# Layer 1's MoE: the four experts of a block side by side instead of two and two

## The chip, the core and the metric

The kernel runs on one core of one Trainium2 chip. The metric is the device time of one execution, in microseconds (us). Engines by their names in the profile: TensorE (PE; its weight loads are PEld), VectorE (DVE), ScalarE (ACT), GpSimd (POOL), SyncE (SP, whose queue issues nearly all loads).

## The reference, cut to what matters

Two layers run over 256 context and 256 latent tokens of width 1024. Each has a mixer (attention and a state-space scan) and then a mixture of experts: a router takes the best of 4 groups and the best 2 of its 8 experts. Only the latent tokens pass through layer 1's MoE, since they alone are the output.

```python
def hier_moe(h, rw1, rb1, rw2, rb2, w_gate, w_up, w_down):
    ...
    y = jnp.zeros_like(h)
    for e in range(N_EXPERTS):                       # 32 experts, EXPERT_FF = 256
        y = y + gate[:, e:e + 1] * ((jax.nn.silu(h @ w_gate[e]) * (h @ w_up[e])) @ w_down[e])
    return y
```

After layer 1 a final RMSNorm follows. All is in f32. An expert has 3 MB of weights, so a layer's MoE reads 96 MB.

## The kernel before, in words

The MoE runs over blocks of experts that together fill 128 slots: 2 experts of 64 slots in layer 0 (16 blocks), 4 experts of 32 slots in layer 1 (8 blocks). Function `moe`, from L1390. For each block b:

- `stage_b` (L1567) gathers the tokens of the block by matmuls with a one-hot matrix `PT` and leaves them transposed, in two halves of the width, in `xgT`.
- `stage_c` (L1596, matmuls on L1610) multiplies by gate and up weights. An expert's gate/up weights come in two tiles of 1 MB, one for each half of the width. The slots of an expert are 32 partitions of the PSUM tile, so its matmuls use 32 columns of TensorE's array. In layer 1, part 0 takes both halves of the experts 0 and 1, alternating between the two, and part 1 both halves of the experts 2 and 3.
- `stage_d1` is SiLU times up, `stage_d2` turns the result, `stage_d3` (L1627, matmuls on L1647; the last block L1638) multiplies by the down weights, one tile of 1 MB for each expert, again two experts at a time.
- `stage_y` and `stage_e` (L1656, L1667) scale by the gate, and scatter back to the tokens by matmuls with `P` (L1673, L1674), times the layer's modulation `g2` (L1677), added to the stream `xs` (L1678). `comb[0]` is the running combine of the block before, and `step` takes one of its four parts.
- `slots` (L1520) makes, once in a layer, the slot tables that `P` and the gates are read from. Its one-hot tile `oh` is on the tag `pT`.

The loop of a block is: d1, gather matrices for block b+2, `P`, `stage_b` of block b+1, d2, `stage_c` part 0 of b+1, d3, y, `stage_c` part 1 of b+1, e. The last block is done in `finish` (L1695), with its down weights in half tiles, all first halves ahead of all second halves. At block 5 of layer 1 stands a branch, `fallback` (L1823, the branch on L1828), which is not taken here.

What sets the order: a planner places the instructions on each engine by its own estimate of durations, unless a `manual_schedule` holds an engine to program order. Layer 0's loop holds TensorE so; layer 1's doesn't (`nullcontext`).

Weights: `seq` lists the tiles of a layer in the order of their use (`add_gu`, `add_dn`, L1398 and L1405); a number such as "tile 16" is a place in this list. Tiles 0 to 3 are loaded ahead during the mixer (`XKEY`, `AHEAD`). Six tiles go in quarters of 256 KB into small buffers that other parts of the kernel leave free (`SMALL`: one letter for each quarter's buffer; `QUARTER` and `qload`, L235). All others rotate over 15 buffers of 1 MB (`LOAD_TAGS`: one R, four W, ten B); such a load waits until TensorE has read the tile that was in its buffer before.

Of the kernel before, what the change touches and what calls it, by code (L numbers as in the profile page):

```python
# [13 lines left out]
D = 1024  # L14
# [17 lines left out]
AHEAD = ((1, "B", 1, 0), (3, "B", 0, 1), (3, "B", 1, 1))  # L32
SMALL = ({2: 'ccxx', 3: 'pppq', 4: 'yyqj', 8: 'mmMM'}, {4: 'pppq', 7: 'yyqj', 6: 'ccxx', 10: 'saom', 12: 'MMlh', 16: 'kwtt'})
# [9 lines left out]
LATE = ((15, 16, 17), ())  # L43
# [4 lines left out]
MAN = ((0, 99), (99, 99))  # L48
# [7 lines left out]
EST = ((0, 0, 0), (1, 1, 1))  # L56
# [26 lines left out]
def _tile_kernel(tc, A, out, dbg=None):  # L83
# [151 lines left out]
    def qload(src, tags, after=None):  # L235
        q = []
        for n, a in enumerate(tags):
# [6 lines left out]
            elif a == "l":  # L244
                t = kc[:, KC["le"][0]:KC["le"][0] + 512]
            elif a == "s":
# [748 lines left out]
    def route_out(l, oT):  # L995
# [394 lines left out]
    def moe(l, R):  # L1390
# [125 lines left out]
        for i in LATE[l]:  # L1516
            load(i, gate if gate is not None else idx[:, 0:1])
# [26 lines left out]
        g2 = {}  # L1544
        if l == 0:
            g2t = big("g2")
        for who in ((1, 0) if l == 0 else (0,)):
            if l == 0:
                g2_ = mod_bcast(l, "g2", who, g2t[:, who * 1024:(who + 1) * 1024])
                g2[who] = [g2_[:, 0:512], g2_[:, 512:1024]]  # L1550
            else:
                g2[who] = []
                for h in range(2):
                    g2[who].append(tw("bm", 2, "g2"))
                    a = 64 + 32 * h + who
                    nc.gpsimd.dma_start(g2[who][h], modd[l, 2][a:a + 1, :].to_broadcast([128, 512]))
# [10 lines left out]
        def stage_b(b):  # L1567
            xg = xgs.pop(b)
            h_ = []
            for kk in range(2):  # L1570
# [22 lines left out]
                step(EST[l][0])  # L1593
            xgT[b] = h_

        def stage_c(b, part):  # L1596
# [4 lines left out]
            if per == 2:  # L1601
                todo = [(part, list(range(2)))]
            else:
# [23 lines left out]
        def stage_d3(b):  # L1627
# [13 lines left out]
            for i0 in range(0, per, 2):  # L1641
                w = {i: get("dn", ex[i], 2) for i in (i0, i0 + 1)}
                for h in range(2):
# [132 lines left out]
        for j in range(1, nT):  # L1776
            V.tensor_scalar(tid[:, j, 0:nb], tid[:, 0, 0:nb], -128.0 * j, None, op0=ALU.add)
# [200 lines left out]
```

## Time and profile before

| what | value |
|---|---|
| median of 3 runs | 1104.37 us (1100.53 to 1105.21) |
| the profiled execution | 1102.8 us, of which the span of its records is 1101.0 us |
| TensorE busy | 1009.9 us, 92% of the span, mean granted clock 0.968 |
| VectorE, ScalarE, GpSimd busy | 608.9, 334.8, 355.0 us |
| moved by DMA | 306.21 MB, mean 278 GB/s |
| layer 1's MoE | about 838 to 1101 us of the span |

The median of the runs is 1.6 us above the profiled execution. "Busy" is the share of time in which an engine has at least one instruction in work; matmuls in different column groups of the array overlap, so a mean duration (about 0.6 us for one of these matmuls) is more than the time that each adds. The granted clock is 1.00 for 2.4 GHz and 0.50 for 1.2 GHz. One f32 matmul of the program is two instructions in the trace, and some records are missing.

### The profile page before, as it was taken

The page shows a single profiled execution, that of the slowest core. Times are in us where ns is not written, and L with a number is a line of the kernel's source. Part 1 is how long each engine was busy: PE and PEld are TensorE (multiplying, and loading weights), DVE is VectorE, ACT ScalarE, POOL GpSimd, SP SyncE. Part 2 cuts the span into 40 slices and gives each one's busy share as a digit, 9 for nine tenths or more (in the row PEclk, how much of TensorE's full clock was granted, in tenths as well). Part 3 has the DMA queues.
Part 4 walks back from the last instruction along what each step waited for, and adds up shares of the span by engine and source line. Part 5 has one row for each costly group of instructions (what it writes and reads, how often), then busy time and mean ns, then how long its engine had stood idle before and what let it go on. Part 6 is the DMA issues. An engine that isn't in the chain of part 4 may idle for free. (4 is left out here: it accounts for less than half of the span.)

```text
span 1101.0 us, 14498 instructions
## 1 busy us (share of the span) xinstructions
PE 1009.9 (92%) x5244; PEld 558.0 (51%) x5244; DVE 608.9 (55%) x1351; ACT 334.8 (30%) x688; POOL 355.0 (32%) x366
## 2 busy tenths in 40 slices
PE   5999999999996999999699889999997999899986
PEld 3778554667674344344244357845775344323321
DVE  4596288875785356556445677749864153222222
ACT  4464344544630111111012075434642111101101
POOL 2130134420562467667636431023311011111121
PEclk9999999999986999999899899999997999999998
DMA  9521577787287997999979164475679699898971
GB/s 375 180 77 52 206 261 257 248 335 311 97 295 293 368 367 318 415 418 404 382 283 418 43 235 155 151 288 212 244 269 329 238 388 420 337 372 356 420 265 39
DMA packets 54675, 306.21 MB, mean 278 GB/s; under 512 B 6168, under 2 KB 7064, under 8 KB 22976
## 3 DMA queue, kind: packets, MB, share of 16 engines
q1 hardware_dynamic: 49120, 288.10, 67.0%
q0 software_dynamic: 4224, 15.21, 4.5%
q10 hardware_dynamic: 1248, 1.86, 0.5%
q8 instruction: 44, 0.72, 0.3%
q14 instruction: 39, 0.32, 0.1%
HBM read 300.89 MB, written 4.26 MB: 277 GB/s over the span
## 5 line engine op out<-in xcount | busy, mean ns | idle before, releaser
L1678 POOL TENSOR_TENSOR xs<-xs,tmp 128x512 f32<-128x512 f32 x144 | 180.2, 1281 | 276.4 <-DVE tmp L1677 276.3
L1610 PE MATMUL bk<-we,xgT 128*64 128x512 f32 (+1 forms) x950 | 242.1, 602 | 0.0
L1610 PEld LDWEIGHTS bk<-we,xgT 128*64 128x64 f32 (+1 forms) x950 | 62.7, 125 | 130.4 <-issue 127.9
L1647 PE MATMUL sc<-we,sa 128*64 128x512 f32 (+1 forms) x430 | 106.2, 600 | 0.1
L1663 DVE SCALAR_TENSOR_TENSOR yl<-sc,gs,yh 128x512 fp32r<-128x512 f32 x46 | 34.3, 748 | 113.2 <-ACT yh L1662 112.6
L1662 ACT ACTIVATE yh<-sc,gs 128x512 fp32r<-128x512 f32 x46 | 31.5, 687 | 210.9 <-PE sc L1647 167.7
L1647 PEld LDWEIGHTS sc<-we,sa 128*64 128x64 f32 (+1 forms) x430 | 31.1, 125 | 58.0 <-issue 56.7
L1677 DVE TENSOR_TENSOR tmp<-md,g 128x512 f32<-128x512 f32 x60 | 41.3, 688 | 29.7 <-POOL xs L1678 18.7
L1677 DVE TENSOR_TENSOR tmp<-py,g 128x512 f32<-128x512 f32 x60 | 41.2, 687 | 24.0 <-PE py L1674 13.2
L1616 ACT ACTIVATE sa<-bk 128x256 f32<-128x256 f32 x24 | 9.2, 383 | 136.1 <-PE bk L1610 126.8
L1578 PEld LDWEIGHTS tp<-PT,h 128*128 128x128 f32 x256 | 33.9, 199 | 28.4 <-issue 12.7
L1578 PE MATMUL tp<-PT,h 128*128 128x128 f32 x256 | 41.5, 300 | 5.0 <-DVE PT L1500 1.7
L770 PE MATMUL sc<-kT,qT 128*128 128x512 f32 (+1 forms) x96 | 45.7, 559 | 0.0
L792 PE MATMUL py<-pT,vt 128*64 128x128 f32 x320 | 43.6, 280 | 1.2 <-DVE oT L821 1.2
L1072 DVE TENSOR_TENSOR lo<-wo,hi 128x512 fp32r<-128x512 f32 x44 | 34.4, 785 | 16.2 <-PE sc L1255 8.6
L1584 DVE TENSOR_SCALAR xgT<-tp,a,sh 128x128 f32<-128x128 f32 x32 | 13.0, 409 | 54.1 <-PE tp L1578 47.5
L1582 ACT ACTIVATE xgT<-tp,sh,a 128x128 f32<-128x128 f32 x32 | 14.6, 457 | 91.0 <-PE tp L1578 85.2
L792 PEld LDWEIGHTS py<-pT,vt 128*64 128x64 f32 x320 | 32.5, 136 | 15.4 <-issue 8.2
L401 PE MATMUL bk<-wh,hH 128*128 128x256 f32 (+1 forms) x128 | 39.8, 311 | 0.2
L403 PE MATMUL bk<-wh,hL 128*128 128x256 f32 (+1 forms) x128 | 38.2, 298 | 1.8 <-DVE hL L382 1.7
L774 ACT ACTIVATE p<-sc,mx 128x512 f32<-128x512 f32 (+1 forms) x48 | 29.4, 612 | 33.2 <-DVE mx L772 23.2
L402 PE MATMUL bk<-wl,hH 128*128 128x256 f32 (+1 forms) x128 | 37.8, 295 | 0.0
(421 smaller groups left out, 2146.5 us busy)
## 6 DMA issues: line engine op xcount, KB each, us to landing
we<-wgu SPq DMA_DIRECT2D x111, 1024.0 KB, 11.1
we<-wdn SPq DMA_DIRECT2D x53, 1024.0 KB, 9.8
wl<-wmod SPq DMA_DIRECT2D x22, 1024.0 KB, 4.9
wl<-wm SPq DMA_DIRECT2D x10, 1024.0 KB, 8.2
wo<-wout SPq DMA_DIRECT2D x8, 1024.0 KB, 5.8
we<-wgu SPq DMA_DIRECT2D x31, 256.0 KB, 5.3
ring<-wgu SPq DMA_DIRECT2D x7, 1024.0 KB, 5.8
wm<-wm SPq DMA_DIRECT2D x6, 1024.0 KB, 12.2
```

Source lines behind the costliest of these rows:

```text
L401: T.matmul(o, a[0], b[0], start=start, stop=False)
L402: T.matmul(o, a[0], b[1], start=False, stop=False)
L403: T.matmul(o, a[1], b[0], start=False, stop=stop)
L770: T.matmul(pm[:, 0:nk], qT[:, e, t * 128:(t + 1) * 128], kT[:, e, 0:nk], start=True, stop=True)
L792: T.matmul(py[e * 64:(e + 1) * 64, 0:128], vts[0][:, k, h * 64:(h + 1) * 64], pT[:, k * 128:(k + 1) * 128], start=(k == 0), stop=(k == nk ...
L1072: eng.tensor_tensor(lo, src, hi.bitcast(F32), op=ALU.subtract)
L1578: T.matmul(p_, R["hres"][t][:, c], xg[j], start=(j == 0), stop=(j == nT - 1))
L1610: T.matmul(pg[c], xgT[b][half][:, k, c], w[i][k], start=(half == 0 and k == 0), stop=(half == 1 and k == 3))
L1647: T.matmul(pd[h][c], aT[:, k, c], w[i][2 * k + h], start=(k == 0), stop=(k == 1))
L1663: V.scalar_tensor_tensor(yl, pd[h], gs[:, b:b + 1], yh.bitcast(F32), op0=ALU.mult, op1=ALU.subtract)
L1677: V.tensor_tensor(tmp, pc, g2[1 if t < 2 else 0][h], op=ALU.mult)
L1678: (eng or (V if EADD[l][n] == "V" or alt and n % 2 else G)).tensor_tensor(xs[:, t, hs_], xs[:, t, hs_], tmp, op=ALU.add)
```

## The change

In layer 1, `stage_c` now takes half `part` of all four experts, k by k, so that four matmuls for four column groups follow each other; `stage_d3` does the same with the down weights; `add_gu` lists the tiles in this order. TensorE is held to program order in layer 1's loop too, with layer 0's loop body. In that order `slots` stands after `stage_c(0, 0)` and before `stage_c(0, 1)`. The small buffers are dealt out anew: tile 6 goes to `MMlk`, tile 12 to `ccxx`, and tile 16 to four quarters of `xs`, rows of context tokens that layer 1 no longer needs; these hold tile 0 first, so tile 16 is loaded after `stage_c(0, 0)`. The one-hot tile moves from `pT` to `bm`, the SiLU tile from `pT` to `xp`, the two loads of `g2` go after `slots`, and the combine takes its PSUM banks in threes.

```diff
-AHEAD = ((1, "B", 1, 0), (3, "B", 0, 1), (3, "B", 1, 1))
-SMALL = ({2: 'ccxx', 3: 'pppq', 4: 'yyqj', 8: 'mmMM'}, {4: 'pppq', 7: 'yyqj', 6: 'ccxx', 10: 'saom', 12: 'MMlh', 16: 'kwtt'})
+AHEAD = ((1, "B", 1, 0), (3, "B", 2, 0), (3, "B", 3, 0))
+SMALL = ({2: 'ccxx', 3: 'pppq', 4: 'yyqj', 8: 'mmMM'}, {4: 'pppq', 7: 'yyqj', 6: 'MMlk', 10: 'saom', 12: 'ccxx', 16: 'XYUZ'})
-LATE = ((15, 16, 17), ())
+LATE = ((15, 16, 17), (16,))
...
+            elif a in "XYUZ":
+                t = xs[:, a in "XY", (a in "YZ") * 512:(a in "YZ") * 512 + 512]
...
-                    oht.append(tw("pT", 2, "oh"))
+                    oht.append(tw("bm" if l else "pT", 2, "oh"))
...
         def add_gu(b, part):
             ex = list(range(b * per, (b + 1) * per))
-            if per == 2:
-                seq.extend(("gu", e, part) for e in ex)
-            else:
-                seq.extend(("gu", e, h) for h in range(2) for e in ex[2 * part:2 * part + 2])
+            seq.extend(("gu", e, part) for e in ex)
...
         def stage_c(b, part):
...
-            if per == 2:
-                todo = [(part, list(range(2)))]
-            else:
-                todo = [(h, [2 * part, 2 * part + 1]) for h in range(2)]
-            for half, which in todo:
-                w = {i: get("gu", ex[i], half) for i in which}
-                for k in range(4):
-                    for i in which:
-                        c = slice(i * cap, (i + 1) * cap)
-                        T.matmul(pg[c], xgT[b][half][:, k, c], w[i][k], start=(half == 0 and k == 0), stop=(half == 1 and k == 3))
-                    step(EST[l][1])
+            w = [get("gu", e, part) for e in ex]
+            for k in range(4):
+                for i in range(per):
+                    c = slice(i * cap, (i + 1) * cap)
+                    T.matmul(pg[c], xgT[b][part][:, k, c], w[i][k], start=(part == 0 and k == 0), stop=(part == 1 and k == 3))
...
-            sa = tw("pT", 2, "sa")
+            sa = P.tile([128, 520], F32, tag="xp", name="sa", bufs=2)[:, 0:512] if l else tw("pT", 2, "sa")
...
-            for i0 in range(0, per, 2):
-                w = {i: get("dn", ex[i], 2) for i in (i0, i0 + 1)}
-                for h in range(2):
-                    for k in range(2):
-                        for i in (i0, i0 + 1):
-                            c = slice(i * cap, (i + 1) * cap)
-                            T.matmul(pd[h][c], aT[:, k, c], w[i][2 * k + h], start=(k == 0), stop=(k == 1))
-                        step(EST[l][2])
+            w = [get("dn", e, 2) for e in ex]
+            for h in range(2):
+                for k in range(2):
+                    for i in range(per):
+                        c = slice(i * cap, (i + 1) * cap)
+                        T.matmul(pd[h][c], aT[:, k, c], w[i][2 * k + h], start=(k == 0), stop=(k == 1))
...
-                pc = (py_() if n % 2 else md_()) if l else (md_, py_, bk)[n % 3]()
+                pc = (md_, py_, bk)[n % 3]()
...
-        man = nullcontext() if l else tc.manual_schedule(engines=ME)
-        man.__enter__()
-        stage_b(0)
-        stage_c(0, 0)
-        slots()
...
+        with tc.manual_schedule(engines=ME):
+            stage_b(0)
+            stage_c(0, 0)
+            for i in LATE[l] if l else ():
+                load(i)
+            slots()
...
+            if l:
+                gate2()
+            stage_c(0, 1)
+            for b in range(nb - 1):
+                stage_d1(b)
...
                 stage_p(b)
                 stage_b(b + 1)
                 step(2)
```

## Rows read from the trace of the kernel before

**Rows 1.** Page, part 2: busy tenths of TensorE and GB/s, 40 slices of 27.5 us.
```profile
PE   5999999999996999999699889999997999899986
...
GB/s 375 180 77 52 206 261 257 248 335 311 97 295 293 368 367 318 415 418 404 382 283 418 43 235 155 151 288 212 244 269 329 238 388 420 337 372 356 420 265 39
```

**Rows 2.** Windows of 10 us: busy us and (instructions) per engine, granted clock, DMA share, GB/s.
```profile
860.00:870.00 10.00, 10.00 (x57) 4.22 (x58) 1.85 (x6) 3.11 (x5) 0.00 (x0) 1.00 0.32 116
870.00:880.00 10.00, 9.93 (x61) 3.08 (x56) 2.13 (x7) 0.38 (x1) 0.00 (x0) 1.00 0.67 263
880.00:890.00 10.00, 10.00 (x66) 5.61 (x60) 6.55 (x27) 2.87 (x6) 0.00 (x0) 1.00 0.78 299
...
900.00:910.00 10.00, 10.00 (x55) 2.65 (x45) 1.50 (x2) 1.39 (x3) 0.00 (x0) 1.00 1.01 421
...
940.00:950.00 10.00, 8.81 (x32) 2.78 (x30) 4.71 (x9) 1.74 (x3) 4.02 (x4) 1.00 0.86 334
950.00:960.00 10.00, 8.94 (x44) 3.69 (x41) 1.67 (x4) 0.84 (x2) 0.99 (x1) 1.00 0.81 322
960.00:970.00 10.00, 9.65 (x49) 3.72 (x49) 1.85 (x6) 1.37 (x3) 0.00 (x0) 1.00 0.64 255
...
990.00:1000.00 10.00, 10.00 (x56) 2.93 (x52) 0.00 (x0) 0.61 (x1) 0.00 (x0) 1.00 0.65 244
...
1050.00:1060.00 10.00, 9.07 (x42) 2.45 (x40) 0.85 (x2) 0.38 (x1) 0.00 (x0) 1.00 0.94 354
```

**Rows 3.** Waits of the SP load queue, 700 to 1101: us in total, times, longest.
```profile
SPq L141 <- PE bk L1610: 118.4, 33, 11.7
SPq L141 <- PE sc L1647: 41.9, 16, 9.3
...
SPq L1828 <- SPq L1828: 9.8, 3, 5.3
```

**Rows 4.** Timeline of the SP load queue: start, us, instructions.
```profile
867.11 1.50 SPq L141 DMA_DIRECT2D we<-wdn  x2
```

**Rows 5.** Timeline of TensorE: runs of matmuls in pairs and in fours.
```profile
644.15 2.78 PE L303 MATMUL md<-wm,kc 128*32 128x512 f32 x24
...
904.59 5.32 PE L1610 MATMUL bk<-we,xgT 128*32 128x512 f32 x24
...
1083.44 1.94 PE L1638 MATMUL sc<-we,sa 128*32 128x512 f32 x16
```

**Rows 6.** Timeline of TensorE: gather, slot and combine matmuls.
```profile
838.25 4.20 PE L1578 MATMUL tp<-PT,h 128*128 128x128 f32 x16 [1.74 <-DVE PT L1500]
...
858.30 2.00 PE L1578 MATMUL tp<-PT,h 128*128 128x128 f32 x12
...
884.77 1.11 PE L1532 MATMUL md<-rv,oh 128*128 128x64 f32 x8
...
911.30 0.39 PE L1674 MATMUL md<-yl,P 128*128 128x512 f32 x1
...
911.53 0.40 PE L1674 MATMUL py<-yl,P 128*128 128x512 f32 x1
```

**Rows 7.** Windows of 1 us, columns as in rows 2.
```profile
830.00:831.00 1.00, 0.55 (x3) 0.41 (x2) 0.38 (x2) 1.00 (x2) 0.00 (x0) 0.50 0.87 313
...
843.00:844.00 1.00, 1.00 (x3) 0.18 (x2) 0.00 (x0) 0.00 (x0) 0.00 (x0) 0.82 1.03 434
...
1067.00:1068.00 1.00, 0.56 (x2) 0.32 (x3) 0.90 (x2) 0.00 (x0) 0.62 (x1) 1.00 0.10 31
```

**Rows 8.** Timeline of VectorE, in brackets the idle time before.
```profile
844.65 0.86 DVE L1584 TENSOR_SCALAR xgT<-tp,a,sh 128x128 f32<-128x128 f32 x2 [3.91 <-PE tp L1578]
...
881.06 0.92 DVE L1130 TENSOR_SCALAR rv<-key,k,kc 128x32 f32<-128x32 f32 x4 [3.28 <-PE sc L1647]
```

**Rows 9.** Timeline of ScalarE and TensorE in the last block.
```profile
1081.32 0.38 ACT L1616 ACTIVATE sa<-bk 128x256 f32<-128x256 f32 x1 [15.40 <-PE bk L1610]
...
1088.51 1.94 PE L1638 MATMUL sc<-we,sa 128*32 128x512 f32 x14
```

More of the change, by code (lines that the diff above doesn't have):

```diff
@@ L47 @@
 WK = 5
-MAN = ((0, 99), (99, 99))
 GB = 0
@@ L55 @@
 SPOS = (13, 12)
-EST = ((0, 0, 0), (1, 1, 1))
 ET = mybir.EngineType
@@ L1515, in moe @@
                 pin(G.tensor_copy(gate, iota[:, 0:1]))
-        for i in LATE[l]:
+        for i in LATE[l] if l == 0 else ():
             load(i, gate if gate is not None else idx[:, 0:1])
@@ L1544, in moe, with gate2 @@
         g2 = {}
-        if l == 0:
[L1546 to L1550, printed above, removed]
-            else:
-                g2[who] = []
-                for h in range(2):
-                    g2[who].append(tw("bm", 2, "g2"))
-                    a = 64 + 32 * h + who
-                    nc.gpsimd.dma_start(g2[who][h], modd[l, 2][a:a + 1, :].to_broadcast([128, 512]))
+        def gate2():
+            if l == 0:
+                g2t = big("g2")
+                for who in (1, 0):
+                    g2_ = mod_bcast(l, "g2", who, g2t[:, who * 1024:(who + 1) * 1024])
+                    g2[who] = [g2_[:, 0:512], g2_[:, 512:1024]]
+                return
+            g2[0] = []
+            for h in range(2):
+                g2[0].append(tw("bm", 2, "g2"))
+                nc.gpsimd.dma_start(g2[0][h], modd[l, 2][64 + 32 * h:65 + 32 * h, :].to_broadcast([128, 512]))
+        if l == 0:
+            gate2()
         fg = xs[:, 0]
@@ L1592, in stage_b @@
                 h_.append(x_)
-                step(EST[l][0])
             xgT[b] = h_
@@ L1640, in stage_d3 @@
                 return
-            for i0 in range(0, per, 2):
-                w = {i: get("dn", ex[i], 2) for i in (i0, i0 + 1)}
-                for h in range(2):
-                    for k in range(2):
-                        for i in (i0, i0 + 1):
-                            c = slice(i * cap, (i + 1) * cap)
-                            T.matmul(pd[h][c], aT[:, k, c], w[i][2 * k + h], start=(k == 0), stop=(k == 1))
-                        step(EST[l][2])
+            w = [get("dn", e, 2) for e in ex]
+            for h in range(2):
+                for k in range(2):
+                    for i in range(per):
+                        c = slice(i * cap, (i + 1) * cap)
+                        T.matmul(pd[h][c], aT[:, k, c], w[i][2 * k + h], start=(k == 0), stop=(k == 1))
             yield
@@ L1769, in finish @@
             fin.update(heads=heads_, low=low, high=high, add=add, mean=mean, rx=rx)
-        man = nullcontext() if l else tc.manual_schedule(engines=ME)
-        man.__enter__()
-        stage_b(0)
-        stage_c(0, 0)
-        slots()
-        for j in range(1, nT):
-            V.tensor_scalar(tid[:, j, 0:nb], tid[:, 0, 0:nb], -128.0 * j, None, op0=ALU.add)
-        stage_c(0, 1)
-        for b in range(nb - 1):
-            stage_d1(b)
-            if b + AH[l] < nb:
-                gather(b + AH[l])
-            if lastl and b == 2:
-                nc.gpsimd.dma_start(fg, A["fg"].to_broadcast([128, D]))
-            if b == FB[l]:
-                drain(comb[0])
-                fallback(l, R, gt4, cmi)
-            if l == 0:
+        with tc.manual_schedule(engines=ME):
[4 more added lines that the diff above has]
+            slots()
+            for j in range(1, nT):
+                V.tensor_scalar(tid[:, j, 0:nb], tid[:, 0, 0:nb], -128.0 * j, None, op0=ALU.add)
+            if l:
+                gate2()
+            stage_c(0, 1)
+            for b in range(nb - 1):
+                stage_d1(b)
+                if b + AH[l] < nb:
+                    gather(b + AH[l])
+                if lastl and b == 2:
+                    nc.gpsimd.dma_start(fg, A["fg"].to_broadcast([128, D]))
+                if b == FB[l]:
+                    drain(comb[0])
+                    fallback(l, R, gt4, cmi)
                 stage_p(b)
@@ L1798, in moe @@
                 if b == nb - 2:
-                    comb[0] = stage_e(b, alt=True)
+                    comb[0] = stage_e(b, alt=not lastl)
                 stage_c(b + 1, 1)
@@ L1802, in moe @@
                     comb[0] = stage_e(b)
-                continue
-            stage_p(b)
-            stage_b(b + 1)
-            stage_d2(b)
-            stage_c(b + 1, 0)
-            drain(stage_d3(b))
-            drain(comb[0])
-            stage_y(b)
-            if b == nb - 2:
-                comb[0] = stage_e(b)
-            stage_c(b + 1, 1)
-            if b < nb - 2:
-                comb[0] = stage_e(b)
-        man.__exit__(None, None, None)
         drain(comb[0])
```

1 line of the change is left out of this document (removed).

## The prediction

> **What bounds the kernel now.** I read the slices of the page first: in the last quarter, which is layer 1's MoE, TensorE is busy nine tenths or more nearly everywhere, while the transfer rate swings between 238 and 420 GB/s [rows 1]. So the stage runs close to two limits at once, and the next question is which of them makes the other wait. The windows of 10 us answer it: full windows carry 421 GB/s, and between them stand 116, 263, 299, 334, 322, 255 and 244 GB/s with TensorE at 8.8 to 10.0 us of 10 [rows 2]. The list of waits of the queue that issues the loads says why: over layer 1 it waited 118.4 us for gate/up matmuls and 41.9 us for down matmuls, that is for buffers that TensorE had not yet read [rows 3]. TensorE frees buffers a little too slowly, the transfers pause, and when the last weights have landed at about 1067.2 [rows 7] TensorE still has 33.8 us of work up to the end of the span at 1101.0. TensorE sets the end, with the transfers 10% behind it.
>
> The work of one block (four experts) can be put in numbers. TensorE: an f32 matmul is two instructions, so gate/up is 4 x 8 x 2 = 64 and down 4 x 4 x 2 = 32, 96 in all. In pairs, 24 take 5.32 us, 0.222 us each [rows 5], so 21.3 us. The other matmuls of a block: 32 gather instructions at 2.00/12 = 0.167 us, 5.3 us; 8 combine instructions at 0.23 us (the step from one row to the next), 1.8 us; the two turns of the activation, some 0.4 us by estimate [rows 6]. Sum 28.9 us. Transfers: 12 tiles of 1.049 MB at 421 GB/s are 29.9 us. Two nearly equal loads, coupled by 15 rotating buffers.
>
> **Four side by side.** The changed loops issue, for each k, the four experts into the four column groups. The same shape in the same order exists already: the modulation matmuls of layer 1 (four groups of 32 columns, 128x512 f32) run 24 in 2.78 us, 0.116 us each; in the last block 16 down matmuls take 1.94 us, 0.121 us each [rows 5]. So 96 x 0.116 = 11.1 us in place of 21.3, and a block costs TensorE 11.1 + 7.5 = 18.7 us. That is 10.2 us less for each of 8 blocks, 82 us, but it can't all be kept: the transfers still need 29.9 us a block. From then on they are the bound, and what can be won is (1) an earlier first release of buffers, (2) the pauses of the transfers, (3) TensorE's backlog after the last weight.
>
> **(1) First release.** Loads up to tile 25 need nothing from the MoE but block 0's gate/up matmuls; the transfers run dry after 860 (116 GB/s to 870 [rows 2]), and the next loads go out at 867.11 [rows 4], when block 1's first gate/up matmuls free their buffers. In the new order: the first 16 gather instructions end at 842.4 as now (838.25 + 4.20, at the low clock); 16 more, 2.7 us; 32 gate/up, 3.7 us, to 848.8; the slot matmuls, 1.1 us [rows 6]; 32 gate/up, 3.7 us, to 853.6; the next block's gather, 5.3 us; the turn, 0.4; 32 gate/up, 3.7, to 863.0. That is 4.1 us before 867.11.
> The slot matmuls are moved ahead of the second gate/up half, and in program order TensorE has to wait for their inputs. Behind them stand that half, the next gather and all later work. Their VectorE work is three times four instructions, 0.92 us a time [rows 8], 2.8 us, in a gap of 3.91 us that VectorE has just then; the changed buffer for the one-hot tile is free once the routing is done, where the old one was held by a weight piece. Cost taken: 0. If VectorE places it after the gap: up to 3 us on TensorE, part of it before the transfers run dry, so under 3 us on the end. If these inputs are early: no gain either, as the queue stands on block 1.
> Tile 16 (four quarter loads) moves behind the first gate/up half: it goes out at 848.8 instead of before 838 and is first read at about 866.7. The loads queued behind it on SP (tiles 21 to 25) need those same matmuls, so they lose nothing: 0, bounded by -1 and, if it heads the queue before tiles 19 and 20, +5 us. The two gate loads of 256 KB on POOL's queue go behind the slot work; the adds queued behind them start after 870, and their first reader is block 1's combine: 0.
>
> **(2) Pauses.** At TensorE's 18.7 us against 29.9 us, a group of four tiles is read within 3.7 us of its last landing, and 11 more buffers, 27 us of transfer, are free or filling by then. So the pauses caused by buffers go. From the windows, (420 - rate)/420 x 10 us: 3.7 and 2.9 (870 to 890), 2.0, 2.3 and 3.9 (940 to 970), 14.8 us together [rows 2]. The pause of 4.2 us at 990 to 1000 stays: the load queue waits there for itself at the fallback's branch, 9.8 us in three waits [rows 3], until its loads have landed. It could also shrink (-4) or grow by some microseconds if fewer loads are queued around it (+4). The final gain's 512 KB load falls into the full stretch now, 0.52/0.42 = 1.2 us more. Transfers end at 1067.2 - 4.1 - 14.8 + 1.2 = 1049.5.
>
> **(3) Tail.** The last 8 half tiles (4.19 MB) at 354 GB/s [rows 2] take 11.8 us, so the last gate/up weights are in at 1037.7. Then 32 gate/up instructions, 3.7 us at full clock or 7.4 at half, and from there what stands now between the last SiLU at 1081.32 and the end, 19.7 us [rows 9]: 1061.1 to 1064.8. By the other way, from the last down tile: the last group of down matmuls starts at 1088.51, 12.5 us before the end [rows 9]: 1049.5 + 12.5 = 1062.0. I take 1063, a tail of 13.5 us for 33.8, a gain of 20.3.
>
> The remaining edits (combine banks, the SiLU tile's buffer, other small pieces of constants for tiles 6 and 12) change no count of instructions or bytes; they lie beside a TensorE with 11 us to spare in a block, and without that cover would cost at most a wait of about 1 us in a block. Layer 0 keeps its path: 0.
>
> **Sum.** 4.1 + 14.8 - 1.2 + 20.3 = 38.0 us. The profiled execution took 1102.8 us (span 1101.0), so 1064.8; the median of the runs is 1.6 us above it, so **1066 us**.
>
> **Against it: the clock.** With transfers as the bound, TensorE works some 3.7 us on a group and then waits for the next, about 10 us apart. Its granted clock stood at 0.50 (1.2 of 2.4 GHz) as it ran out of work at 830, and was on its way back to 1.00 only at 843, some 5 us into steady work that began at 838 [rows 6, 7]. So many groups will run at 1.2 GHz. A block wholly at that level: 96 x 0.232 = 22.3, gather 2 x 4.20 = 8.4, combine 3.7, turn 0.9, together 35.3 us, over the transfers' 29.9. But a TensorE that is then busy all the time gets its clock back, as at 843. I expect a mixture under 30 us, which costs nothing until the tail (the 7.4 above). The Trainium skill speaks against this change here: "TensorE: Matmul & The Clock Gate", section "HAM oscillation — how this bites in real kernels", tells of a kernel whose bursts of matmuls were shorter than its wait for the next weights and which was throttled again at every step. The fall at 830 agrees with it; by it alone the sum would be that of rivals B or D.
>
> **Rivals.**
> A, the forecast: transfers bound, 1066, by itself 1056 to 1077. Chance 0.66.
> B, a clock that stays low part of the time, or loads held up in SP's order, so that half of the gains (1) to (3) is lost: 38.0/2 = 19, so 1085. For: the fall at 830. Against: 27 us of buffers. Chance 0.18.
> C, the change doesn't do what it says: the four don't overlap, or buffers stay as late. Then TensorE keeps 28.9 us a block, the pauses stay, and only the 4.1 us of the first release are left: 1100. Against: both rows of four. Chance 0.07.
> D, slower: the low clock throughout together with program order, in which a wait for SiLU or a combine bank can't be filled with other matmuls. From the first group of block 1 (863.0) six blocks follow, then a tail of about 25 us (19.7 and 5 for the clock). The time passes 1101.0 + 5.5 when a block costs (1106.5 - 25 - 863.0)/6 = 36.4 us, that is 35.3 and over 1.1 us of exposed waits. At 3 us of waits: 863.0 + 6 x 38.3 + 25 = 1117.8 span, 1121 by the median. For: the low clock. Against: busy TensorE regained its clock, and layer 0, which is ordered in this way already, carried 415 to 418 GB/s in three of its slices [rows 1]. Chance 0.09.
>
> **How the numbers follow.** What a measurement can tell here is about 0.5%, 5.5 us. Faster: A, B and a third of C's spread, 0.86; same: the rest of C, 0.05; slower: D, 0.09. The range takes A with the unknown costs (-4 for the branch and some microseconds of tail, down to 1056) and B with a few microseconds (1090); left out are C, D and the thin ends, under 0.2.
>
> **What would show it.** Right: in the profile after, 24 gate/up matmuls in some 2.8 us; transfers over 410 GB/s from about 865 to 1045 but for one pause at the branch; load waits on matmuls shrunk to a fraction; TensorE idle for several microseconds before groups, waiting for loads, with its clock at 0.50 in many windows; the last load in at about 1050 and the end 13 to 16 us later. Wrong: pauses of the transfers with the load queue waiting for matmuls (B, C, D), TensorE busy over 90% at a granted clock near 0.5 (D), or 0.22 us for each matmul (C).

## The result, and the profile after

The changed kernel takes **1077.47 us** (median; 1076.52 to 1078.54) against 1103.09 us before, measured beside it: a ratio of 0.976 with a 95% interval of 0.973 to 0.980. The profiled execution took 1077.21 us with a span of 1075.4 us. That is 25.6 us faster, inside the range (1056 to 1090), but 11.5 us above the predicted 1066: of a forecast gain of 38 us, two thirds came.

The page of the kernel after, parts 2 and 5 (busy tenths and GB/s in 40 slices, now of 26.9 us; then one group: instructions, busy us and mean ns, idle time before them and what ended it):

```profile
PE   5999999999996999999969979999999678877785
...
GB/s 380 188 42 76 143 312 253 255 301 267 220 178 284 378 360 405 317 418 417 360 375 329 268 79 194 236 156 258 178 326 236 229 335 395 420 419 387 391 418 208
...
L1578 PE MATMUL tp<-PT,h 128*128 128x128 f32 x256 | 56.4, 362 | 32.7 <-DVE xgT L1584 18.9
```

Against [rows 1] the last quarter has changed sides: TensorE shows sixes, sevens and eights where it had nines, and the transfers run at 387 to 420 GB/s in six slices running. The group is the gather of the tokens, and it has grown: the kernel before spent 41.5 us on the same 256 instructions and waited 5.0 us ahead of them.

Windows of 10 us of the kernel after (busy us and instructions of TensorE, its weight loads, VectorE, ScalarE, GpSimd; granted clock, DMA share, GB/s), as in [rows 2]:

```profile
850.00:860.00 10.00, 8.98 (x56) 4.23 (x60) 2.10 (x11) 2.12 (x3) 0.35 (x1) 0.70 0.29 75
860.00:870.00 10.00, 7.28 (x55) 4.13 (x48) 3.45 (x15) 1.75 (x4) 0.18 (x1) 1.00 0.97 353
870.00:880.00 10.00, 9.42 (x89) 3.38 (x91) 2.89 (x8) 1.83 (x3) 0.00 (x0) 1.00 0.65 250
...
920.00:930.00 10.00, 9.73 (x87) 2.70 (x80) 4.18 (x6) 1.37 (x2) 3.15 (x3) 1.00 1.01 418
...
990.00:1000.00 10.00, 5.46 (x19) 3.36 (x18) 5.64 (x12) 0.84 (x2) 4.94 (x4) 0.80 0.63 249
1000.00:1010.00 10.00, 7.75 (x30) 5.76 (x34) 1.66 (x4) 1.37 (x3) 0.00 (x0) 0.50 1.01 423
...
1050.00:1060.00 10.00, 7.86 (x50) 2.16 (x50) 1.03 (x3) 0.75 (x2) 1.91 (x2) 1.00 1.04 382
1060.00:1070.00 10.00, 6.22 (x24) 1.85 (x24) 4.70 (x8) 3.92 (x11) 4.74 (x8) 1.00 0.04 14
```

The middle is as forecast: full transfers, one pause at the branch, and the last weights in at about 1060.4, 15.0 us before the end (33.8 before). The start is not: by windows of 1 us the transfers stand still (under 50 GB/s) from 850 to 856, while the load queue waits for block 0's gate/up matmuls, and from 874 to 876, while it waits for block 1's. That is 8 us, hardly less than the 10 us of the kernel before (862 to 868 and 878 to 882), although TensorE's matmuls now take half the time. The load queue's own waits from 690 on (total, times, longest), which answer [rows 3]:

```profile
SPq L139 <- PE bk L1604: 49.0, 11, 17.4
SPq L139 <- DMA we<-wgu: 39.0, 22, 2.1
...
SPq L1807 <- SPq L1807: 19.6, 2, 17.1
SPq L256 <- PE bk L1604: 17.5, 4, 15.7
...
SPq L139 <- PE sc L1639: 4.4, 4, 2.2
```

118.4 us of waiting for gate/up matmuls became 49.0, of which one wait is 17.4, and 41.9 us for down matmuls became 4.4; most other waits are now for transfers, so the queue is ahead of them. The row of L256 holds tile 16's wait, 15.7 us at the head of the queue. The queue's wait at the branch (L1807) has doubled, from 9.8 to 19.6 us, but the transfers lose no more there than before: 249 GB/s in the window of 10 us against 244.

**Four marks in time.** They cut layer 1's MoE into pieces that can be compared between kernels. ScalarE's SiLU runs once in a block, when the last gate/up matmul of the block is done, so its rows are the best ruler of the stage. First SiLU of block 1 and of the last block, in the kernel before and then in the kernel after (start, us):

```profile
882.85 0.38 ACT L1616 ACTIVATE sa<-bk 128x256 f32<-128x256 f32 x1 [9.36 <-PE sc L1647]
```

```profile
882.38 0.38 ACT L1609 ACTIVATE sa<-bk 128x256 f32<-128x256 f32 x1 [2.77 <-PE bk L1604]
...
1055.47 0.38 ACT L1609 ACTIVATE sa<-bk 128x256 f32<-128x256 f32 x1 [10.04 <-PE bk L1604]
```

With [rows 6] (first gather instruction at 838.25) and [rows 9] (last SiLU at 1081.32), the kernel before took 44.6 us from the first gather to block 1's SiLU, 198.5 us for the six blocks from there, and 19.7 us to the end. The kernel after began its gather at 840.82 and took 41.6, 173.1 and 19.9 us. In the kernel before, though, the first mark is late: this SiLU waited for down matmuls (L1647), while the last gate/up matmuls of its block were done at 876.5.

```profile
870.77 5.74 PE L1610 MATMUL bk<-we,xgT 128*32 128x512 f32 x25
```

Counted from there, its start took 38.3 us and its six blocks 204.8. So the whole gain was made in the six blocks, 25.4 us by SiLU and 31.7 by the gate/up matmuls; the start gave 3.0 us by the first count and lost 3.3 by the second; and the part ahead of the MoE took 2.6 us longer. That part is not the change's: in the runs below its end lies anywhere from 835.4 to 845.8, whatever the kernel. The shift arises far ahead of the edits: the same early ScalarE instruction in the kernel before, the kernel after and the run e2 below:

```profile
56.62 0.22 ACT L835 ACTIVATE sact<-kd 128x16 f32<-128x16 f32 x1
```

```profile
59.10 0.22 ACT L835 ACTIVATE sact<-kd 128x16 f32<-128x16 f32 x1
```

```profile
54.50 0.22 ACT L835 ACTIVATE sact<-kd 128x16 f32<-128x16 f32 x1
```

So 2.5 of the 2.6 us are there after 59 us, and e2's profiled execution is ahead by 2.1 us at the same place; what makes it so is open. For this reason kernels are best compared from their own first gather on. All runs of this study on the same ruler:

| kernel | median us | first gather | to SiLU of block 1 | six blocks | last SiLU to end |
|---|---|---|---|---|---|
| before (by gate/up matmuls) | 1103.1 | 838.25 | 44.6 (38.3) | 198.5 (204.8) | 19.7 |
| after | 1077.5 | 840.82 | 41.6 | 173.1 | 19.9 |
| e1_pairs | 1084.7 | 837.59 | 51.2 | 173.2 | 19.9 |
| e2_planner | 1065.0 | 835.46 | 33.3 | 173.8 | 19.9 |
| e3_drain | 1068.9 | 842.47 | 29.4 | 176.1 | 19.8 |
| e8_pairs_planner | 1071.1 | 836.78 | 38.6 | 172.4 | 19.8 |
| e12_twice | 1086.9 | 838.51 | 43.3 | 186.5 | 19.9 |
| e13_down_thrice | 1103.4 | 836.63 | 47.2 | 196.2 | 19.9 |
| e4_no16 | 1079.4 | 838.87 | 46.4 | 173.8 | 20.1 |
| e5_extra_after | 1098.0 | 837.18 | 45.9 | 194.2 | 19.8 |
| e6_drain_branch1 | 1064.7 | 840.24 | 29.8 | 174.0 | 19.9 |
| e10_planner_branch1 | 1070.1 | 845.77 | 32.8 | 172.9 | 19.9 |
| e7_best | 1062.8 | 835.42 | 29.9 | 171.8 | 20.1 |

### The profile page after: what moved, and what is told of

It is laid out like the page before. It is cut to its first block, busy times and chain, and to the rows that moved or that the text cites. A ratio compares the mean times of both kernels' runs of the same rounds, so it can differ in the third digit from the quotient of the medians.

```text
span 1075.4 us, 14508 instructions
## 1 busy us (share of the span) xinstructions
PE 954.0 (89%) x5244; PEld 556.7 (52%) x5244; DVE 610.3 (57%) x1351; ACT 335.1 (31%) x688; POOL 354.6 (33%) x366
## 5 line engine op out<-in xcount | busy, mean ns | idle before, releaser
L1604 PE MATMUL bk<-we,xgT 128*64 128x512 f32 (+1 forms) x942 | 189.6, 610 | 7.2 <-DMA we<-wgu 7.2
L1604 PEld LDWEIGHTS bk<-we,xgT 128*64 128x64 f32 (+1 forms) x942 | 51.4, 126 | 104.9 <-issue 90.2
L1639 PE MATMUL sc<-we,sa 128*64 128x512 f32 (+1 forms) x432 | 87.0, 599 | 1.1 <-DMA we<-wdn 1.1
L1578 PE MATMUL tp<-PT,h 128*128 128x128 f32 x256 | 56.4, 362 | 32.7 <-DVE xgT L1584 18.9
L1578 PEld LDWEIGHTS tp<-PT,h 128*128 128x128 f32 x256 | 43.4, 245 | 49.3 <-DVE xgT L1584 26.3
L1668 DVE TENSOR_TENSOR tmp<-md,g 128x512 f32<-128x512 f32 x60 | 41.3, 688 | 26.7 <-POOL xs L1669 22.4
L1639 PEld LDWEIGHTS sc<-we,sa 128*64 128x64 f32 (+1 forms) x432 | 26.6, 125 | 53.0 <-issue 50.4
L1668 DVE TENSOR_TENSOR tmp<-py,g 128x512 f32<-128x512 f32 x53 | 36.4, 686 | 23.9 <-PE py L1665 13.0
L774 ACT ACTIVATE p<-sc,mx 128x512 f32<-128x512 f32 (+1 forms) x48 | 29.4, 612 | 33.7 <-DVE mx L772 26.8
## 6 DMA issues: line engine op xcount, KB each, us to landing
we<-wdn SPq DMA_DIRECT2D x53, 1024.0 KB, 12.2
wm<-wm SPq DMA_DIRECT2D x6, 1024.0 KB, 12.2
```

The lines of the kernel that those rows point to most:

```text
L1578: T.matmul(p_, R["hres"][t][:, c], xg[j], start=(j == 0), stop=(j == nT - 1))
L1604: T.matmul(pg[c], xgT[b][part][:, k, c], w[i][k], start=(part == 0 and k == 0), stop=(part == 1 and k == 3))
L1668: V.tensor_tensor(tmp, pc, g2[1 if t < 2 else 0][h], op=ALU.mult)
```

## The experiments

The theory after the result: TensorE no longer bounds the six blocks, transfers do; what is missing was lost at the start, in the gather, which in program order waits for its own evacuations. The rivals: the loss is the clock's or the side-by-side matmuls' own; or the gain comes from the new load order and hand-out of small tiles, not from TensorE.

**What the gather does in program order.** TensorE's timeline of the kernel after (start, us, in brackets the idle time before and what ended it), and two rows of the load queue:

```profile
842.51 1.22 PE L1578 MATMUL tp<-PT,h 128*128 128x128 f32 x4 [0.50 <-DVE xgT L1584]
844.28 1.23 PE L1578 MATMUL tp<-PT,h 128*128 128x128 f32 x4 [0.55 <-ACT xgT L1582]
...
864.06 0.71 PE L1578 MATMUL tp<-PT,h 128*128 128x128 f32 x4 [0.50 <-DVE xgT L1584]
...
875.18 3.62 PE L1639 MATMUL sc<-we,sa 128*32 128x512 f32 x32
```

```profile
855.34 3.32 SPq L256 DMA_DIRECT2D xs<-wgu  x4
...
875.38 0.81 SPq L139 DMA_DIRECT2D we<-wdn  x2
```

Four gather instructions fill a quarter of a PSUM tile; then TensorE stands 0.50 to 0.60 us until VectorE or ScalarE has copied that quarter out, and goes on in the next quarter of the same tile. Block 0's gather so ran from 840.82 to 853.39, 12.6 us, block 1's from 862.84 to 871.41, 8.6 us. The first load into a buffer of block 1 went out at 875.38, the last row. The fours themselves (matmuls for the four experts side by side) cost what was forecast: 32 in 3.62 us, 0.113 us each, against 0.222 for pairs [rows 5].

**e2: the planner back, fours kept.**

```diff
-        with tc.manual_schedule(engines=ME):
+        with (nullcontext() if l else tc.manual_schedule(engines=ME)):
```

> The changed kernel with layer 1's loop left to the planner, the four side by side in the source. Theory (program order costs the waits between gather matmuls and their evacuations, and the fours bring the gain): the planner fills those waits with other matmuls, so the first release of block 1 comes earlier than 875 and the time is 1066 to 1076 us, if the fours stay together. Rival (program order is what brings the gain): 1090 us or more, with transfers pausing as before the change.

Measured: 1064.95 us (1062.32 to 1068.23), ratio 0.967 (0.962 to 0.972), 1 us below what the theory gave. Its rows of TensorE and of SiLU:

```profile
835.46 4.20 PE L1578 MATMUL tp<-PT,h 128*128 128x128 f32 x16 [1.97 <-DVE PT L1497]
```

```profile
868.75 0.38 ACT L1609 ACTIVATE sa<-bk 128x256 f32<-128x256 f32 x1 [2.75 <-PE bk L1604]
```

Sixteen gather instructions run through in 4.20 us as in [rows 6]; the planner puts other matmuls where the evacuations would be waited for. The start is 8.3 us shorter than in the kernel after, and the six blocks differ by 0.7 us. By the medians program order cost this change 12.5 us; from the first gather to the end of the span it is 7.7 us (234.6 against 226.9), since e2's profiled execution reached the gather 5.4 us earlier. In neither count did program order gain anything.

**e3: program order kept, the wait taken out of the gather.** A half's 16 gather instructions are issued before its four evacuations.

```diff
                             T.matmul(p_, R["hres"][t][:, c], xg[j], start=(j == 0), stop=(j == nT - 1))
-                        if k % 2:
-                            S.activation(x_[:, k], p_, AF.Identity, bias=b2[:, 0, n:n + 1], scale=a2[:, 0, n:n + 1])
...
+                for k in range(4) if l else ():
+                    p_ = pt[:, k * 128:(k + 1) * 128]
...
+                    if k % 2:
+                        S.activation(x_[:, k], p_, AF.Identity, bias=b2[:, 0, n:n + 1], scale=a2[:, 0, n:n + 1])
```

> The changed kernel, but a half's 16 gather instructions are issued before its four evacuations instead of four by four. Theory (the 11 us that the forecast missed are TensorE's waits for the evacuations in its own PSUM tile, 27.8 us in layer 1, and what they delay): a gather of 32 instructions takes 5.3 to 6 us instead of 8.6, in block 0 about 7.5 to 8.5 instead of 12.6; the first release of block 1 comes at 864 to 868 instead of 875; 1066 to 1071 us. Rival (the late release comes from the low clock and the late tile 16, or the end is set by the transfers' rate alone): 1075 to 1079 us.

Measured: 1068.9 us (1064.3 to 1071.18), ratio 0.969 (0.964 to 0.974). TensorE's timeline of e3, then windows of 1 us of e3 and of the kernel after (the third number from the end is the granted clock):

```profile
842.47 6.22 PE L1578 MATMUL tp<-PT,h 128*128 128x128 f32 x32 [1.97 <-DVE PT L1497]
...
856.80 3.84 PE L1578 MATMUL tp<-PT,h 128*128 128x128 f32 x32
```

```profile
846.00:847.00 1.00, 1.00 (x7) 1.00 (x6) 0.74 (x4) 0.29 (x1) 0.00 (x0) 0.50 0.98 365
847.00:848.00 1.00, 1.00 (x9) 1.00 (x8) 0.61 (x3) 0.52 (x2) 0.00 (x0) 0.74 1.01 426
848.00:849.00 1.00, 1.00 (x11) 0.66 (x13) 0.27 (x1) 0.10 (x1) 0.00 (x0) 1.00 0.51 213
```

```profile
855.00:856.00 1.00, 1.00 (x12) 0.24 (x8) 0.00 (x0) 0.26 (x1) 0.00 (x0) 0.50 0.00 0
856.00:857.00 1.00, 1.00 (x16) 0.35 (x12) 0.00 (x0) 0.00 (x0) 0.00 (x0) 0.99 0.53 119
```

The same 32 instructions take 6.22 us instead of 12.6, and 3.84 instead of 8.6. In block 0 six waits sum to 3.3 us of the 6.3 between them. Most of the rest is the clock: all 32 at the low level would be 8.4 us by [rows 6] (2 x 4.20), 2.2 over e3's; some 0.8 us stays without a name. In e3 TensorE works without a break from 842.47 and is back at 1.00 at 848; in the kernel after, with a break at every quarter, it stays at 0.50 (1.2 of 2.4 GHz) until 856. e3's first release load goes out at 864.86, 22.4 us after its first gather, where the kernel after needs 34.6. The gather came out shorter than expected (5.3 to 6 and 7.5 to 8.5 us), the release and the time where the theory had them. With that one wait gone, program order is as good as the planner from the first gather on (225.3 us of span in e3, 226.9 in e2; 234.6 after). The start is 12.2 us shorter and the six blocks 3.0 us longer than in the kernel after, so that the start carries the loss is shown.

**e1: pairs in the new order.**

```diff
-            for k in range(4):
-                for i in range(per):
...
+            for i0 in range(0, per, 2):
+                for k in range(4):
+                    for i in (i0, i0 + 1):
...
```

(The matmul below stays as it is; the down stage is changed in the same way.)

> The changed kernel with one thing undone: gate/up and down matmuls go in pairs of experts again (program order, order of loads and small buffers as changed). Theory (four side by side makes TensorE quick enough for the transfers to become the bound): a block then costs TensorE 21.3 us for 96 matmuls, some 8.6 for the gather with its waits and 2.2 for the rest, 32.1 us, over the transfers' 29.9; the first release of block 1 comes at about 885 instead of 875 and six blocks of 32 follow: 1095 to 1108 us, transfers pausing again. Rival (program order and the small buffers bring the gain): 1073 to 1082 us, transfers still over 410 GB/s from 890 on.

Measured: 1084.74 us (1083.62 to 1094.48), ratio 0.987 (0.981 to 0.993): between the two expectations, and the table says where. The six blocks did not slow down at all, 173.2 us; only the start did, by 9.6 us. TensorE's timeline explains the blocks, first of the kernel before, then of e1:

```profile
902.88 7.04 PE L1610 MATMUL bk<-we,xgT 128*32 128x512 f32 x32
...
969.59 5.40 PE L1647 MATMUL sc<-we,sa 128*32 128x512 f32 x32
```

```profile
900.02 4.09 PE L1605 MATMUL bk<-we,xgT 128*32 128x512 f32 x26
903.53 0.62 PE L1641 MATMUL sc<-we,sa 128*32 128x512 f32 x1
...
903.94 0.60 PE L1605 MATMUL bk<-we,xgT 128*32 128x512 f32 x2
...
912.35 0.71 PE L1578 MATMUL tp<-PT,h 128*128 128x128 f32 x4
```

In the kernel before, two experts' first and second halves, 32 instructions in the same two column groups, stand behind each other and take 7.04 us, 0.22 each. Its down matmuls, 16 in one pair of column groups and then 16 in the other, are quicker already: 5.40 us, 0.169 each. In e1 a pair in columns 0 and 1 is followed by a pair in columns 2 and 3, and the two overlap: 26 instructions start within 3.5 us, gate/up (bk) and down (sc) run interleaved, and the 96 instructions of the block, by the program's count, fill 900.02 to 912.35, 12.3 us or 0.128 each. This agrees with the Trainium skill, "TensorEngine Tiling (Array Packing)", section "Key Properties", by which different tiles of the array can execute in parallel; what the rows add is that instructions several places apart in the stream do so. So e1 was no return to 21 us a block, and could not show what 21 us cost. In its start the gather of block 1 fell to the low clock as well and took 11.0 us (863.52 to 874.50), where the kernel after needed 8.6.

**e8: e1 and e2 together, pairs under the planner.**

> The kernel of e2 (the change's load order, buffers and small tiles; layer 1 placed by the planner) with the pairs of e1. In e1's trace two pairs behind each other in other column groups overlapped, 96 instructions of a block in 12.3 us (900.02 to 912.35). Theory (not the number side by side but the columns standing next to each other in the instruction stream set TensorE's time, so such pairs cost a block only 1 to 2 us more than fours, under the transfers' 30 us): 1064 to 1072, near e2's 1065. Rival (pairs cost 0.22 us an instruction wherever the planner moves them, 21 us a block, as in the kernel before): 1085 to 1103.

Measured: 1071.11 us (1069.41 to 1077.53), ratio 0.973 (0.969 to 0.977), as the theory had it. Pairs in the order that the new load sequence allows are 6 us from fours (1064.95), and 32 us from the kernel before, which had pairs under the planner too. These 32 us hold the order of the column groups, but also the new load sequence, small tiles and buffers; e12 and e13 ask which of them it is.

**e12 and e13: TensorE's work put back.** On e2, the gate/up matmuls of layer 1's blocks 1 to 7 and the down matmuls of its blocks 0 to 6 are issued twice (e12), the down matmuls three times (e13). The sums, and so the output, are then others; only the time is of interest.

```diff
-            for k in range(4):
+            ks = (0, 0, 1, 1, 2, 2, 3, 3) if l and b else (0, 1, 2, 3)
+            for n, k in enumerate(ks):
...
+            ks = (0, 0, 1, 1) if l else (0, 1)
...
-                for k in range(2):
+                for n, k in enumerate(ks):
...
```

In e13 the second line reads

```diff
-            ks = (0, 0, 1, 1) if l else (0, 1)
+            ks = (0, 0, 0, 1, 1, 1) if l else (0, 1)
```

> The kernel of e2 (the change, but layer 1's instructions placed by the planner as before), in which each f32 matmul of four side by side of blocks 1 on is issued twice (the sums are counted twice, so the output is another). TensorE's matmuls of a block then take 192 x 0.113 = 21.7 us, about what the pairs took before (21.3), while load order, small tiles, buffers and transfers are the change's. Theory (what TensorE needs for a block is what the change cut, and it carries the gain): the gain goes back almost wholly, 1092 to 1108 us, with pauses of the transfers in which the load queue waits for matmuls and a tail of about 30 us. Rival (the new load order and hand-out of small tiles carry a good part): 1068 to 1085, the transfers still near 420 GB/s from 870 on.

> The kernel of e12, in which the down matmuls are issued three times (sums counted as often, so the output is another): 224 x 0.11 = 25 us, and with the 6 us of gather and combine about 31 us of TensorE a block, where e12's trace shows a period of 27.0 us in the full stretch (901.62 to 928.66) and the kernel before one of 31.2 us (896.84 to 928.06). Theory (TensorE's time for a block is all that the change cut; e12 at 27.0 was only a smaller dose): 1098 to 1112, at or above the kernel before. Rival (the new load order and hand-out of small tiles hold the 12 us by which e12's transfers ended earlier than before's, whatever TensorE needs): 1087 to 1095.

Measured: e12 1086.93 us (1086.19 to 1089.87), ratio 0.986 (0.983 to 0.988), between the two expectations: 22 of 38 us went back. With e13, the larger dose, it is 1103.35 us, ratio **1.0004** (0.9985 to 1.0023), as its theory had it. SiLU in e13, and its load queue's waits:

```profile
853.45 0.38 ACT L1610 ACTIVATE sa<-bk 128x256 f32<-128x256 f32 x1 [5.63 <-PE bk L1605]
883.82 0.38 ACT L1610 ACTIVATE sa<-bk 128x256 f32<-128x256 f32 x1 [6.18 <-PE bk L1605]
914.30 0.38 ACT L1610 ACTIVATE sa<-bk 128x256 f32<-128x256 f32 x1 [6.12 <-PE bk L1605]
```

```profile
SPq L139 <- PE bk L1605: 113.4, 15, 18.3
SPq L139 <- PE sc L1641: 45.9, 6, 11.1
```

A block now lasts 30.4 to 30.5 us, TensorE's time, and the waits are those of [rows 3] again, 113.4 and 45.9 against 118.4 and 41.9. Load order, small tiles and buffers are the change's in all of it. So the rival falls as an account of the whole: TensorE's time for a block is enough to take the whole gain back.

How large a dose matches the kernel before, two sets of windows tell. First about one block of the kernel before, of e8 and of e12, each in a stretch in which TensorE was busy all the time; then the whole of layer 1's MoE in the kernel before, in e12 and in e13:

```profile
896.84:928.06 31.22, 31.22 (x151) 11.95 (x147) 9.53 (x19) 3.59 (x7) 5.05 (x4) 1.00 1.01 419
```

```profile
875.42:898.04 22.62, 22.62 (x156) 11.21 (x156) 11.14 (x20) 4.49 (x9) 5.13 (x4) 1.00 1.00 413
```

```profile
901.62:928.66 27.04, 27.04 (x238) 11.23 (x234) 10.30 (x18) 3.57 (x7) 5.18 (x4) 1.00 1.01 420
```

```profile
838.25:1101.00 262.75, 239.76 (x1116) 89.35 (x1116) 71.61 (x166) 33.27 (x66) 40.34 (x37) 0.97 0.79 317
```

```profile
838.51:1088.10 249.59, 232.00 (x1788) 92.99 (x1788) 75.43 (x162) 33.49 (x66) 41.27 (x38) 0.97 0.84 337
```

```profile
836.63:1099.90 263.27, 251.19 (x2012) 101.68 (x2012) 76.96 (x162) 33.39 (x66) 41.42 (x38) 0.97 0.81 320
```

The first window holds 8 gather instructions of another block and the second 17; without them, at 0.167 us each, a block is some 29.9 us in the kernel before and some 20 in e8 (estimates), against 27.0 in e12 and 30.5 in e13. Over the whole MoE the kernel before kept TensorE busy for 239.8 us, between e12's 232.0 and e13's 251.2. On a straight line between e12 and e13 the kernel before would lie some 3 us lower by the first count and some 8 by the second. So 3 to 8 of the 38 us may belong to the load order and the small tiles after all; the rest goes with TensorE's time.

Nor is there a sharp knee at the transfers' 29.9 us a block. With some 20, 27.0 and 30.5 us a block, e8, e12 and e13 lie 6, 22 and 38 us above e2: much of the gain is lost while TensorE's block is still shorter than the transfers'. In e12 most of the loss is work that is left behind the last weight (33.6 us from the last landing at 1054.5 to the end; 16.8 in e2). An account that fits, and that no run tests: the tiles up to 25 of 96 wait for no block after block 0, so TensorE has eight blocks to do while the transfers have some six, and it sets the end unless it needs less than about 6 x 29.9 / 8 = 22 us for a block (an estimate from these rows).

**e5: more to transfer.** On the kernel after, ten loads of 512 KB that nothing reads, two in each of blocks 2 to 6.

```diff
+                for _ in range(2 if l and b >= 2 else 0):
+                    nc.sync.dma_start(xs[:, 1], A["wgu"][1, 0, 0][:, 0:1024])
```

> The changed kernel with 5 MB of loads more, which nobody reads: two of 512 KB into a free part of xs in each of the blocks 2 to 6 of layer 1, on the same queue. Theory (transfers are the bound there): 5.24 MB at 420 GB/s, 12.5 us more, 1087 to 1093 us. Rival (TensorE with its waits is the bound, the transfers have slack): 1077 to 1082 us.

Measured: 1098.01 us (1093.56 to 1099.45), ratio 0.995 (0.993 to 0.997), 20.5 us over the kernel after, where 5.24 MB at 420 GB/s are 12.5. One row of the load queue's waits from 850 on gives the rest:

```profile
SPq L1783 <- DMA xs<-wgu: 71.0, 5, 15.9
```

The second of each two loads waits for the first, since both write one buffer, and all loads of weights queue behind it. The time lies above both expectations. That more to transfer lengthens the six blocks (194.2 for 173.1) agrees with transfers as their bound, but the experiment brought in a wait of its own, so it does not show it by itself; the windows at 417 to 421 GB/s do.

**e4: tile 16 in a rotating buffer.** Tile 16 is taken out of the lists of small and late tiles (SMALL and LATE).

> The change, but tile 16 is no longer cut into four quarters: it takes a rotating buffer in its turn. Theory (tile 16 is read late, and its four loads at the head of the load queue only wait for what the next tiles need as well): 1 MB less can be under way before block 1 frees its buffers, 1.05 MB / 420 GB/s = 2.5 us later: 1078 to 1082 against 1077.5. Rival (the loads behind tile 16 are held up by it, up to 5 us, the empty transfers at 850 to 856 being its doing): 1070 to 1075.

Measured: 1079.44 us (1072.8 to 1080.96), ratio 0.977 (0.973 to 0.981): not to be told from the kernel after, and where the theory had it. The start is 4.8 us longer; its first release load stands at 878.31 and its transfers stand still around 855 and 875 as well, so tile 16, which waits at the head of the queue until 855.34, holds nothing up that could have gone.

**e10 and e6: the branch in block 1,** on e2 and on e3.

```diff
-FB = (11, 5)
+FB = (11, 1)
```

> The kernel of e2 with the fallback's branch in block 1 instead of block 5. Theory (transfers are the bound, so their pause at the branch is paid in full, 10 us at 221 of 420 GB/s = 4.7 us; in block 1 the load queue has little under way and waits for buffers anyway): 1059 to 1062 against 1065. Rival (the pause only moves, or the earlier branch holds the combine of block 0): 1065 or more.

> The kernel of e3 (program order, each half of the gather issued whole before its evacuations) with the fallback's branch in block 1 instead of block 5. Theory (the pause of the transfers at the branch, 10 us at 241 of 420 GB/s = 4.3 us, is on the path since transfers bound): 1063 to 1066 against 1068.9. Rival (the pause only moves): 1068 to 1071.

Measured: e10 1070.11 us (1063.63 to 1073.11), ratio 0.969 (0.964 to 0.973); e6 1064.66 us (1061.44 to 1065.87), ratio 0.965 (0.961 to 0.968). One went up by 5 us, into its rival's range, and one down by 4, into its theory's; both intervals overlap those of e2 and e3. e10's profiled execution began its gather at 845.77, 10.3 us after e2's, so its median says little of the branch. On the ruler the six blocks became shorter by 0.9 and 2.1 us, less than the 4.7 and 4.3 expected. A window of 10 us of e6:

```profile
870.00:880.00 10.00, 6.54 (x46) 5.15 (x49) 6.96 (x17) 1.70 (x4) 5.48 (x5) 1.00 0.79 301
```

The pause did not vanish, it moved here, where the transfers had just begun to run full. What the branch's place is worth, if anything, stays open within some 5 us.

**e7: e6, and tile 16 in one load of 1 MB** instead of four of 256 KB.

```diff
-            if i in SMALL[l]:
+            if l and i == 16:
+                v = xs[:, 0:2].rearrange("p t c -> p (t c)")
+                nc.sync.dma_start(v, src)
+                q = [v[:, n * 512:(n + 1) * 512] for n in range(4)]
+            elif i in SMALL[l]:
```

> The kernel of e6 (program order, halves of the gather drained late, branch in block 1) with tile 16 loaded into its place in one piece of 1 MB instead of four of 256 KB. Theory (the transfers run at about 200 GB/s while the four quarters and little else are under way, 856 to 859 in the trace of the change, so one piece is in 1 to 2 us earlier, before the first release): 1062 to 1065 against 1064.7. Rival (the load queue stands on block 1's buffers anyway): 1064 to 1066.

Measured: 1062.84 us (1059.01 to 1065.69), ratio 0.963 (0.960 to 0.967). It is the fastest kernel seen here, 3.7% under the one before and 1.4% under the changed one; against e6, e2 and e3 the intervals overlap, so the single load and the branch have no proven share in that. The time is inside the theory's range, 1 us below the rival's. What is proven is the part that these kernels have in common: fours, without the gather's wait.

## Why the prediction was right, and where it was off

The predicted time on the ruler: its first release at 863.0 is followed by down and gate/up matmuls, 3.7 us each, so SiLU of block 1 at 870.4, 32.2 us after the first gather; its end of span at 1063.0, less 19.7, puts the last SiLU at 1043.3, so 172.9 us for six blocks. Measured: 41.6 and 173.1.

- **Four side by side.** Forecast 0.116 us an instruction, measured 0.113. TensorE's block fell far below the transfers' 29.9 us as forecast, and that is what mattered: with the work put back to 30.5 us a block the gain is gone to 0.04% (e13). The block of the kernel before was priced at 28.9 us, where its trace gives some 29.9. Too narrow was the reading that the kernel before owed its 0.222 us to pairs as such. It owed them to pairs that follow each other in the same columns; pairs that change columns come to 0.128 (e1), and the fours as such are worth 6 to 7 us by the medians, under the planner or without it (3.9 and 9.7 us from the first gather on).
- **(1) First release.** This step failed. It put the release at 863.0, 24.7 us after the first gather; it came at 875.38, 34.6 us after, where the kernel before had needed 28.9 us (867.11). A gain of 4.1 us was forecast and 5.7 us were lost. The term that was mis-sized is the gather: 6.9 us for block 0 and 5.3 us for block 1 were taken from runs that the planner had made (0.167 us an instruction, [rows 6]), while the time line itself was drawn in program order. There each quarter waits for its evacuation, in block 0 the clock stays low besides, and the terms measured 12.6 and 8.6 us: 9.0 us of the 9.8. Gate/up matmuls at the low clock gave 1.1 us more, of which smaller terms took 0.3 back. The prediction named a wait for SiLU or a combine bank as the price of program order (rival D), and not this one. Without the wait the step comes out: 22.4 us in e3.
- The slot matmuls cost nothing, as taken: they begin at 858.24, right behind the gate/up half. Tile 16 cost nothing either, though it did head the queue for 15.7 us (e4).
- **(2) Pauses.** Right. From the first release to the last landing the transfers took 185.0 us against 200.1 before, 15.1 less; forecast were 13.6 (14.8 less 1.2). From 910 to 990 every window holds 417 to 421 GB/s, and the pause at the branch is there, 249 GB/s at 990 to 1000 against 244 before. The last landing, forecast for 1049.5, came at 1060.4, 10.9 us late; the release had been 12.4 us late, 9.8 by step (1) and 2.6 since this execution reached the MoE later.
- **(3) Tail.** Right: 15.0 us for 13.5, and 19.9 us from the last SiLU for 19.7.
- **The clock.** Right for the blocks: the windows after show 0.50 at 1000 to 1010 and 0.65 to 1.00 elsewhere, with the transfers at 423 GB/s all the same. The trace agrees with the rule quoted there from the Trainium skill, "TensorE: Matmul & The Clock Gate", section "HAM oscillation — how this bites in real kernels", in that the clock falls. The falls cost nothing in the blocks, where the transfers are the bound. Missed was the start, where TensorE is the bound: the clock came back 15 us after the first gather, in e3, without the gather's breaks, 5.5 us after it.
- **Rivals.** The time is inside the stated range, but just past the bounds that A gave itself (1056 to 1077), and nearer to B's 1085 than to A's 1066: that the range held it, it owes to the width that B had added. Of B's mechanism only a part came, and only at the start: the clock stayed low until 856. Loads were held up in SP's order too, behind tile 16, but that cost nothing (e4). The gains (2) and (3) came almost whole. C and D fell with the rows of fours and six blocks of 28.9 us.

## What to carry to other kernels

Price a piece of work in the order in which it will be issued: a row taken from a planner's schedule holds no wait that program order would expose, and a loop of "fill a quarter, copy it out" in one PSUM tile exposes one each time. When two resources need nearly the same time for a block, do not look for the knee where the two times are equal: here more than half of the gain was gone at 27.0 us of TensorE a block, with the transfers at 29.9. Once the transfers run full, the start of the stage, in which they do not yet, is what is left to gain.

## What the runs showed of the hardware

- Matmuls of 32 columns overlap with others several places on in the stream if these lie in other column groups: 96 instructions in pairs took 12.3 us in e1, where 32 in one pair of column groups took 7.04 us in the kernel before.
- With breaks of 0.5 to 0.6 us at every fourth instruction the granted clock stayed at 0.50 from 840 to 856; in e3, with the same instructions and no breaks from 842.47 on, it was at 1.00 at 848. The same breaks did not bring it down at once: in the next gather of the kernel after, 862.84 to 871.41, it stayed at 1.00; in that of e1 it fell at 867.
- From the first gather on, the five kernels with fours and no such wait lie between 221.8 and 226.9 us (e2, e3, e6, e7, e10), while the moment of the first gather moved by 10 us between profiled executions (835.4 to 845.8). Between before, after and e2 most of the shift is there at 57 us, in code that the edits do not touch (54.50 to 59.10); its cause is open.
